# Background transfers of the state-space parameters on POOL's queue, and the kernel table's store one step later

## The chip, the cores and the metric

The kernel runs on one core of one Trainium2 chip. The time is device microseconds of one execution; the median of several runs is compared. The engines of the core are PE (matrix products), DVE and ACT (element-wise work), POOL (the GpSimd engine) and SP, whose only work here is to issue DMA transfers. Each engine has its own instruction queue and works through it in order; semaphores hold an instruction until what it needs is there.

## The reference

One step of a two-layer encoder for 512 prompt frames and 64 sample frames. Layer 0 has attention and a short convolution, layer 1 a diagonal state-space mixer (S5); each layer also has two SwiGLU blocks and a cross attention. The change touches only the parameters of the state-space mixer:

```python
def ssm_mixer(h, w_in, a_re, a_im, b_re, b_im, c_re, c_im, log_dt, d_skip, w_glu, h0_re, h0_im):
    u32 = (h @ w_in).astype(f32)
    ug = u32.reshape(B, S, SSM_GROUPS, SSM_GROUP)              # 64 groups of 16 channels
    lam = lax.complex(a_re, a_im)                              # (64 groups, 64 states)
    a_bar = jnp.exp(lam * jnp.exp(log_dt)[:, None])
    b_bar = ((a_bar - 1.0) / lam)[..., None] * lax.complex(b_re, b_im)
    c_mat = lax.complex(c_re, c_im)
    # h_t = a_bar * h_(t-1) + b_bar u_t ;  y_t = Re(c_mat h_t) + d_skip * u_t
    ...
    val, gate = jnp.split(jax.nn.gelu(y) @ w_glu, 2, axis=-1)
    return val * jax.nn.sigmoid(gate), h_last.real, h_last.imag
```

The kernel works through the frames in blocks of eight. For that it needs tables made of `a_bar`, `b_bar` and `c_mat` only: WIN (what eight inputs add to the state), T (what the inputs of a block give to the outputs of the same block, with `d_skip` on its diagonal), WOUT (what the state gives to eight outputs) and TAB (rotations). They do not depend on `x`.

## The kernel before

All activations lie feature by frame in SBUF, 576 frames wide. The work is a list of *steps* made by hand. A step names the weight pieces (granules) that it needs; `run_steps` issues the load of each granule on SP (`wraw`, three buffers, up to three ahead), lets ACT round it to a high part `wh` and DVE take the rest `wl`, and then emits the step's matrix products on PE, three passes of 128x288 each. A full granule is 512 KB.

Beside the steps runs a list of *background pieces*, `self.bg`. Each has a cost in microseconds; after every step, `run_steps` gives a credit of 6 per granule and emits pieces while credit is left. So the order of all instructions on every queue is fixed when the program is written; what an engine does at which time is settled by the semaphores alone.

`s5_params` makes the background pieces for the tables, during the first SwiGLU block:

- `start` and `to_rows` compute powers of `a_bar`; PE transposes them (L1518).
- The *WIN phase*: `win_load` brings factors `f` from a DRAM scratch, in 32 transfers of 128 KB (16 partitions each); `win_calc(i)`, for i from 0 to 7, loads `b` (512 KB, one buffer) and makes a complex product of six operations on POOL (L1402 to L1407), with the result in `w` (two buffers); `win_store` writes `w` to WIN in DRAM. The pools of this phase are closed at its end.
- The *kernel phase*: `ca_begin` opens new pools in the same memory, loads `x`, `bx` (four transfers of 512 KB, L1552 and L1553) and `dd`, and clears `gp`; `bst` makes the input matrix in `bx`. Then for each i: `ca_calc(i)` (POOL and DVE make `ca`), `local(i)` (PE multiplies, L1586; ACT copies into `gp`; DVE adds the diagonal), `ca_store` (WOUT) and `t_store` (eight transfers from shifted windows of `gp` to T).
- The rotation phase (TAB), on DVE and POOL.

Before the change every DMA of the kernel is issued by SP, the weight loads among them. A store to DRAM and a later load of memory that it read are tied by semaphores; each transfer uses one of eight semaphores of its kind, and waits until the transfer that used it eight transfers before has landed.

Of the kernel before, what the change touches and what calls it, by code (L numbers as in the profile page):

```python
# [9 lines left out]
F32 = mybir.dt.float32  # L10
# [67 lines left out]
class Kernel:  # L78
# [1305 lines left out]
    def s5_params(self):  # L1384

        nc, a = self.nc, self.a
        V, S_, P_ = nc.vector, nc.scalar, nc.gpsimd
        dr = self.dram
        d = self.s5d = {
            "F": dr.tile([2, 8, 4096], F32, name="s5f"),  # L1390
            "TAB": dr.tile([8, 128, 2 * 592], F32, name="s5tab"),
            "R8": dr.tile([128, SG], F32, name="s5r8"),
            "WIN": dr.tile([8, 128, 1024], F32, name="s5win"),
            "T": dr.tile([8, 128, 1024], F32, name="s5t"),
            "WOUT": dr.tile([8, 128, 1024], F32, name="s5wout"),
        }
        st = {}
# [3 lines left out]
        def cmul(e, o_r, o_i, ar, ai, br, bi, t):  # L1401
            e.tensor_tensor(o_r, ar, br, op=ALU.mult)  # L1402
            e.tensor_tensor(t, ai, bi, op=ALU.mult)
            e.tensor_tensor(o_r, o_r, t, op=ALU.subtract)
            e.tensor_tensor(o_i, ar, bi, op=ALU.mult)  # L1405
            e.tensor_tensor(t, ai, br, op=ALU.mult)
            e.tensor_tensor(o_i, o_i, t, op=ALU.add)  # L1407
# [115 lines left out]
        def win_load(hf, q):  # L1523
            if hf == 0 and q == 0:
                st["wp"] = self.phase_pool(st, "s5w")
                st["wp2"] = self.phase_pool(st, "s5w2", 2)
            if q == 0:
                st["f", hf] = [st["wp2"].tile([128, 32, G], F32, tag=f"f{c}", name="f") for c in range(2)]
            f, c = st["f", hf], q // 2
            for s in range(4 * (q % 2), 4 * (q % 2) + 4):  # L1530
                nc.sync.dma_start(f[c][16 * s:16 * s + 16].rearrange("p g n -> p (g n)"),
                                  d["F"][c, s:s + 1, hf * 2048:(hf + 1) * 2048].broadcast_to((16, 2048)))

        def win_calc(i):
            pl = st["wp"]
            b = pl.tile([128, 2, 8, G], F32, tag="b", name="b")
            nc.sync.dma_start(b, a["ssm_bw"][i].rearrange("p (c g n) -> p c g n", c=2, g=8))
            fr, fi = (f[:, (i % 4) * 8:(i % 4) * 8 + 8] for f in st["f", i // 4])
            w = st["w", i] = st["wp2"].tile([128, 8, 2, G], F32, tag="w", name="w")
            t = pl.tile([128, 8, G], F32, tag="t", name="t")  # L1540
            cmul(P_, w[:, :, 0], w[:, :, 1], b[:, 0], b[:, 1], fr, fi, t)

        def win_store(i):
            nc.sync.dma_start(d["WIN"][i], st["w", i].rearrange("p g c n -> p (g c n)"))


        def ca_begin():
            pl = st["wp"] = self.phase_pool(st, "s5o")
            st["x"] = [pl.tile([128, G, 16], F32, name=f"x{c}") for c in range(2)]
            st["bx"] = [pl.tile([128, G, 16], F32, name=f"bx{c}") for c in range(2)]  # L1550
            for c in range(2):
                nc.sync.dma_start(st["x"][c].rearrange("p g n -> p (g n)"), a["ssm_cx"][c])  # L1552
                nc.sync.dma_start(st["bx"][c].rearrange("p g n -> p (g n)"), a["ssm_bx"][c])  # L1553
            st["dd"] = pl.tile([16, G], F32, name="dd")
            nc.sync.dma_start(st["dd"], a["ssm_dd"])
            st["wp2"] = self.phase_pool(st, "s5o2", 2)
            st["gp"] = pl.tile([16, 8, 240], F32, name="gp")
            P_.memset(st["gp"], 0.0)

        def bst():  # L1560
            b0, b1 = st["bx"]
# [5 lines left out]
        def ca_calc(i):  # L1567
            pl = st["wp"]
            ca = st["ca", i] = st["wp2"].tile([128, 8, 9, 16], F32, tag="ca", name="ca")
            t = st["wp2"].tile([128, 8, 9, 16], F32, tag="cat", name="cat")  # L1570
            gs = slice(8 * i, 8 * i + 8)
            sh = (128, 8, 9, 16)
            x = [v[:, gs].unsqueeze(2).broadcast_to(sh) for v in st["x"]]
            p = [st["sr"][:, 9 * c:9 * c + 9, gs].rearrange("p k g -> p g k").unsqueeze(3).broadcast_to(sh) for c in range(2)]
            P_.tensor_tensor(ca, x[0], p[0], op=ALU.mult)
            V.tensor_tensor(t, x[1], p[1], op=ALU.mult)
            V.tensor_tensor(ca, ca, t, op=ALU.add)

        def ca_store(i):
            nc.sync.dma_start(d["WOUT"][i].rearrange("p (g n) -> p g n", g=8), st["ca", i][:, :, 1:].rearrange("p g k c -> p g (k c)"))  # L1580

        def local(i):
            ps = self.ps("ps_g")
            pf = ps[:16].rearrange("p b (g n) -> p (b g) n", g=4)
            for g in range(8):
                nc.tensor.matmul(pf[:, g], st["bx"][0][:, 8 * i + g], st["ca", i][:, g, 0:8].rearrange("p k c -> p (k c)"),  # L1586
                                 start=True, stop=True)
            gp = st["gp"]
            S_.activation(gp[:, :, 112:], pf, AF.Copy)
            dg = st["wp"].tile([16, 8, 16], F32, tag="dg", name="dg")  # L1590
            V.tensor_tensor(dg, self.ident[:16, :16].unsqueeze(1).broadcast_to((16, 8, 16)),
                            st["dd"][:, 8 * i:8 * i + 8].unsqueeze(2).broadcast_to((16, 8, 16)), op=ALU.mult)
            V.tensor_tensor(gp[:, :, 112:128], gp[:, :, 112:128], dg, op=ALU.add)

        def t_store(i):
            for s in range(8):
                nc.sync.dma_start(d["T"][i, 16 * s:16 * s + 16].rearrange("p (g n) -> p g n", n=128),
                                  st["gp"][:, :, 112 - 16 * s:240 - 16 * s])


        def rot_begin(hf):
# [36 lines left out]
        add = lambda cost, fn=lambda: None: pieces.append((cost, fn))  # L1638
# [9 lines left out]
        for hf in range(2):  # L1648
            if hf == 0:
                for q in range(4):  # L1650
                    add(2, lambda q=q: win_load(0, q))
            for i in range(4 * hf, 4 * hf + 4):
                add(8.6, lambda i=i: win_calc(i))
                if hf == 0:
                    add(0, lambda i=i: win_load(1, i))
                if i:
                    add(0, lambda i=i: win_store(i - 1))
        add(5)
        add(0, lambda: win_store(7))
        add(6)  # L1660
        add(2, lambda: (close(2), ca_begin()))
        add(20, bst)
        for i in range(9):
            if i < 8:
                add(5, lambda i=i: ca_calc(i))
            if i:
                add(5, lambda i=i: local(i - 1))
                add(0, lambda i=i: ca_store(i - 1))
                add(1, lambda i=i: t_store(i - 1))
        add(6)  # L1670
        add(2, lambda: close(2))
        for hf in range(2):
# [711 lines left out]
```

## Time and profile before

| | |
|---|---|
| Time, median of 3 runs | 2530.69 us (2527.84 to 2531.97) |
| Profiled execution: its time | 2536.29 us |
| Profiled execution: its span | 2534.3 us |
| PE busy | 2475.3 us (98%) |
| DVE busy | 1781.1 us (70%) |
| ACT busy | 1070.0 us (42%) |
| POOL busy | 764.1 us (30%) |
| Bytes moved, mean rate | 279.98 MB, 110 GB/s |
| Mean granted clock of PE | 0.989 |
| First issue of `f` / first WIN operation on POOL / last store of `w` landed | 115.58 / 138.07 / 228.0 us |

The profile is of one execution. *Busy* counts compute instructions; waiting and the issuing of transfers are not in it. A *wait* row names who waited, on which line, for whom. In a timeline row, what stands in brackets is the idle time of the engine ahead of the instruction, and what ended it. "SPq" is SP's queue of transfers, and the length that it shows for a transfer is that of its issue, not of the transfer.

### The profile page before, as it was taken

The page shows a single profiled execution, that of the slowest core. Times are in us where ns is not written, and L with a number is a line of the kernel's source. Part 1 is how long each engine was busy: PE and PEld are TensorE (multiplying, and loading weights), DVE is VectorE, ACT ScalarE, POOL GpSimd, SP SyncE. Part 2 cuts the span into 40 slices and gives each one's busy share as a digit, 9 for nine tenths or more (in the row PEclk, how much of TensorE's full clock was granted, in tenths as well). Part 3 has the DMA queues.
Part 4 walks back from the last instruction along what each step waited for, and adds up shares of the span by engine and source line. Part 5 has one row for each costly group of instructions (what it writes and reads, how often), then busy time and mean ns, then how long its engine had stood idle before and what let it go on. Part 6 is the DMA issues. An engine that isn't in the chain of part 4 may idle for free.

```text
span 2534.3 us, 45336 instructions
## 1 busy us (share of the span) xinstructions
PE 2475.3 (98%) x18499; PEld 2437.8 (96%) x18499; DVE 1781.1 (70%) x2680; ACT 1070.0 (42%) x1847; POOL 764.1 (30%) x754
## 2 busy tenths in 40 slices
PE   8998999999999999999989999999999999999998
PEld 8998999999899999999989999999999999999998
DVE  5644658667875588886988695965753468787695
ACT  5222222334655454443545352542453355444353
POOL 1566235302420051523334332412310005151431
PEclk9999999999999999999999999999999999999999
DMA  4375653321134322322221322244972222222221
GB/s 156 86 186 183 155 129 114 127 87 36 37 121 134 112 84 75 109 84 100 77 91 61 107 84 100 84 139 157 296 248 85 84 92 87 77 104 86 98 84 63
DMA packets 112560, 279.98 MB, mean 110 GB/s; under 512 B 16304, under 2 KB 45152, under 8 KB 111712
## 3 DMA queue, kind: packets, MB, share of 16 engines
q1 hardware_dynamic: 112352, 277.08, 34.3%
q8 instruction: 145, 2.38, 0.4%
q14 instruction: 63, 0.52, 0.1%
HBM read 245.07 MB, written 31.97 MB: 109 GB/s over the span
## 4 chain that ended last, share of the span: by engine, by line
PE 74%; DVE 13%; ACT 4%; DMA 4%; POOL 2%; issue 2%; SPq 1%; ACTq 0%; DVEq 0%; POOLq 0%
PE banks L396 35%; PE banks L317 26%; DVE wl L144 2%; DVE wl L219 2%; PE banks L657 2%; PE banks L1903 1%; PE banks L2179 1%; PE banks L1284 1%; PE banks L1799 1%; PE banks L1252 1%; ACT wh L138 1%; DMA b<-in_ssm_bw 1%; DMA u<-s5u 1%; DMA wraw<-in_gu 1%; POOL w L1405 1%
## 5 line engine op out<-in xcount | busy, mean ns | idle before, releaser
L138 ACT ACTIVATE wh<-wraw 128x1024 fp32r<-128x1024 f32 (+3 forms) x411 | 351.9, 860 | 330.5 <-PE banks L396 180.7
L219 DVE TENSOR_TENSOR wl<-wraw,wh 128x1024 fp32r<-128x1024 f32 (+2 forms) x264 | 335.4, 1274 | 179.6 <-ACT wh L138 177.4
L396 PE MATMUL banks<-hh,wh 128*128 128x288 f32 x1768 | 380.6, 297 | 2.6 <-ACT hh L138 1.8
L396 PE MATMUL banks<-hh,wl 128*128 128x288 f32 x1768 | 379.7, 296 | 2.5 <-DVE wl L219 2.5
L396 PE MATMUL banks<-hl,wh 128*128 128x288 f32 x1768 | 379.5, 296 | 0.3 <-DVE hl L144 0.3
L317 PE MATMUL banks<-xh,wh 128*128 128x288 f32 x1056 | 312.6, 296 | 0.1
L317 PE MATMUL banks<-xl,wh 128*128 128x288 f32 x1056 | 312.3, 296 | 0.2 <-DVE xl L146 0.2
L317 PE MATMUL banks<-xh,wl 128*128 128x288 f32 x1056 | 312.1, 296 | 0.0
L396 PEld LDWEIGHTS banks<-hh,wh 128*128 128x128 f32 x1768 | 285.8, 189 | 4.0 <-ACT hh L138 2.1
L396 PEld LDWEIGHTS banks<-hh,wl 128*128 128x128 f32 x1768 | 285.9, 189 | 3.0 <-DVE wl L219 3.0
L396 PEld LDWEIGHTS banks<-hl,wh 128*128 128x128 f32 x1768 | 285.8, 189 | 0.5 <-DVE hl L144 0.5
L396 PE MATMUL banks<-xh,wh 128*128 128x288 f32 x1232 | 268.3, 299 | 10.6 <-ACT wh L138 9.7
L396 PE MATMUL banks<-xh,wl 128*128 128x288 f32 x1232 | 266.0, 298 | 5.2 <-DVE wl L219 5.2
L396 PE MATMUL banks<-xl,wh 128*128 128x288 f32 x1232 | 265.1, 297 | 0.0
L317 PE MATMUL banks<-eh,wh 128*128 128x288 f32 x792 | 237.5, 300 | 17.6 <-ACT tb L138 16.7
L317 PE MATMUL banks<-el,wh 128*128 128x288 f32 x792 | 235.4, 297 | 0.0
L317 PE MATMUL banks<-eh,wl 128*128 128x288 f32 x792 | 235.2, 297 | 0.0
L144 DVE TENSOR_TENSOR wl<-ss,wh 128x512 fp32r<-128x512 f32 x264 | 197.3, 760 | 48.9 <-ACT wh L138 48.9
L292 POOL TENSOR_TENSOR ss<-raw 128x512 f32<-128x512 f32 x66 | 103.6, 1570 | 369.6 <-DMA raw<-in_gu 248.4
L396 PEld LDWEIGHTS banks<-xh,wh 128*128 128x128 f32 x1232 | 199.5, 190 | 13.0 <-ACT wh L138 10.2
L396 PEld LDWEIGHTS banks<-xh,wl 128*128 128x128 f32 x1232 | 199.7, 190 | 6.7 <-DVE wl L219 6.6
L317 PEld LDWEIGHTS banks<-xh,wh 128*128 128x128 f32 x1056 | 199.7, 189 | 0.4 <-ACT xh L140 0.4
(536 smaller groups left out, 5432.8 us busy)
## 6 DMA issues: line engine op xcount, KB each, us to landing
wraw<-in_gu SPq DMA_DIRECT2D x110, 512.0 KB
raw<-in_gu SPq DMA_DIRECT2D x66, 512.0 KB
wraw<-in_dn SPq DMA_DIRECT2D x64, 512.0 KB
wraw<-in_dn SPq DMA_DIRECT2D x32, 384.0 KB
wraw<-in_win SPq DMA_DIRECT2D x17, 512.0 KB
wraw<-in_xq SPq DMA_DIRECT2D x16, 512.0 KB
wraw<-in_xk SPq DMA_DIRECT2D x16, 512.0 KB
wraw<-in_xv SPq DMA_DIRECT2D x16, 512.0 KB
```

What stands on the lines that cost most here:

```text
L138: self.nc.scalar.activation(out, in_, AF.Copy)
L144: self.nc.vector.tensor_tensor(out, in_, hi.bitcast(F32), op=ALU.subtract)
L219: self.lo_engine.tensor_tensor(l[:p, :n], t[:p, :n], h[:p, :n].bitcast(F32), op=ALU.subtract)
L292: self.nc.gpsimd.tensor_tensor(t, x, y, op=op)
L317: mm(out, ww[:, ws], xx[:, kk], start=k < 3 and kk == 0 and pi == 0, stop=kk == 3 and pi == 2, skip_group_check=True)
L396: mm(ps[:M, h, :n], ww[:, k * M:(k + 1) * M], xx[:, k0 + k, h * n:(h + 1) * n], start=first and k == 0 and pi == 0, stop=last and k == kt ...
L657: nc.tensor.matmul(ps, ww[:, k * 128:(k + 1) * 128], xx[:, k, c0:c0 + n], start=k == 0 and pi == 0, stop=k == KT - 1 and pi == 2)
L1252: mm(out, x[:, k, t * 128:t * 128 + m], y[:, k], start=k == 0 and pi == 0, stop=k == 1 and pi == 2)
L1284: mm(out, x[:, k, f * 128:(f + 1) * 128], y[:, k, ts], start=k == 0 and pi == 0, stop=k == 1 and pi == 2)
L1405: e.tensor_tensor(o_i, ar, bi, op=ALU.mult)
L1799: mm(pv[:, m], x[:, kk, ms], y[:, k * MEM:(k + 1) * MEM], start=kk == m == pi == 0, stop=kk == 7 and pi == 2 and m == 1)
L1903: mm(ps[:, h, :HF], ww[:, k * 128:(k + 1) * 128], xx[:, k, h * HF:(h + 1) * HF], start=k == 0 and pi == 0, stop=k == 7 and pi == 2)
```

## The change

Three calls in the WIN phase are issued on POOL's queue and no longer on SP's: the loads of `f`, the loads of `b` and the stores of `w`. In the kernel phase there are two buffers `gp` in place of one, cleared both; `t_store(i)` is emitted one round of the loop later, after `ca_calc` of that round and ahead of the next `ca_store`; and `ca_store` is emitted ahead of `local` and no longer behind it.

```diff
 def win_load(hf, q):
-                nc.sync.dma_start(f[c][16 * s:16 * s + 16].rearrange("p g n -> p (g n)"),
+                nc.gpsimd.dma_start(f[c][16 * s:16 * s + 16].rearrange("p g n -> p (g n)"),
                                   d["F"][c, s:s + 1, hf * 2048:(hf + 1) * 2048].broadcast_to((16, 2048)))
 def win_calc(i):
-            nc.sync.dma_start(b, a["ssm_bw"][i].rearrange("p (c g n) -> p c g n", c=2, g=8))
+            nc.gpsimd.dma_start(b, a["ssm_bw"][i].rearrange("p (c g n) -> p c g n", c=2, g=8))
 def win_store(i):
-            nc.sync.dma_start(d["WIN"][i], st["w", i].rearrange("p g c n -> p (g c n)"))
+            nc.gpsimd.dma_start(d["WIN"][i], st["w", i].rearrange("p g c n -> p (g c n)"))
 def ca_begin():
-            st["gp"] = pl.tile([16, 8, 240], F32, name="gp")
-            P_.memset(st["gp"], 0.0)
+            st["gp"] = [pl.tile([16, 8, 240], F32, name=f"gp{c}") for c in range(2)]
+            for c in range(2):
+                P_.memset(st["gp"][c], 0.0)
 # local(i) and t_store(i) use st["gp"][i % 2]
-        for i in range(9):
+        for i in range(10):
             if i < 8:
                 add(5, lambda i=i: ca_calc(i))
-            if i:
+            if i > 1:
+                add(1, lambda i=i: t_store(i - 2))
+            if 0 < i < 9:
+                add(0, lambda i=i: ca_store(i - 1))
                 add(5, lambda i=i: local(i - 1))
-                add(0, lambda i=i: ca_store(i - 1))
-                add(1, lambda i=i: t_store(i - 1))
```

POOL's queue, from the third WIN step to the first operation of the fourth. DMAHW and DMASW are the semaphores of transfers issued by SP and by POOL; `s5win` is WIN in DRAM, `s5f` the scratch of the factors, `in_ssm_bw` the input that `b` is loaded from. Before:

```order
L1402 TENSOR_TENSOR w<-b,f 128x8x64 [waits DMAHW7_49,DMAHW6_49]
L1403 TENSOR_TENSOR t<-b,f 128x512 [waits Pool_49]
L1404 TENSOR_TENSOR w<-w,t 128x8x64 [waits Pool_49]
L1405 TENSOR_TENSOR w<-b,f 128x8x64
L1406 TENSOR_TENSOR t<-b,f 128x512 [waits Pool_49]
L1407 TENSOR_TENSOR w<-w,t 128x8x64 [waits Pool_49]
L1402 TENSOR_TENSOR w<-b,f 128x8x64 [waits DMAHW6_49,DMAHW5_49]
```

The step that begins with only the multiplication ahead of it has six more issues ahead of it now:

```order
L1407 TENSOR_TENSOR w<-w,t 128x8x64 [waits Pool_49]
L1531 DMA f<-s5f 16x2048 x3
L1531 DMA f<-s5f 16x2048 [waits DMASW1_49]
L1544 DMA s5win<-w 128x1024 [waits DMASW2_49]
L1537 DMA b<-in_ssm_bw 128x1024 [waits DMASW3_49]
L1402 TENSOR_TENSOR w<-b,f 128x8x64 [waits DMASW3_49,DMASW2_49]
```

Four loads of `f`, the store of the step before and the load of `b` stand between two steps on POOL; in the last steps, without `f`, there are two.

SP's queue at the passage from the WIN phase to the kernel phase (`in_gu` are weights, `in_ssm_cx` and `in_ssm_bx` the sources of `x` and `bx`). Before:

```order
L1544 DMA s5win<-w 128x1024 [waits Pool_49]
L1537 DMA b<-in_ssm_bw 128x1024 [waits DMAHW5_49,DMAHW0_49,Pool_49]
L188 DMA wraw<-in_gu 128x1024 [waits DMAHW2_49,DVE_49]
L1544 DMA s5win<-w 128x1024 [waits Pool_49]
L188 DMA wraw<-in_gu 128x1024 [waits DMAHW3_49,DVE_49]
L1544 DMA s5win<-w 128x1024 [waits DMAHW4_49,Pool_49]
L188 DMA wraw<-in_gu 128x1024 [waits DMAHW6_49,DVE_49]
L1552 DMA x_2274<-in_ssm_cx 128x1024 [waits DMAHW4_49,DMAHW7_49,DMAHW2_49,DMAHW0_49]
```

The same place now:

```order
L188 DMA wraw<-in_gu 128x1024 [waits DMAHW1_49,DVE_49]
L188 DMA wraw<-in_gu 128x1024 [waits DMAHW2_49,DVE_49]
L1552 DMA x_2274<-in_ssm_cx 128x1024 [waits DMASW4_49,DMASW3_49,DMASW5_49,DMASW2_49,DMASW6_49,DMASW1_49,DMASW7_49,DMASW0_49,Pool_49]
L1553 DMA bx_2276<-in_ssm_bx 128x1024
L1552 DMA x_2275<-in_ssm_cx 128x1024
L1553 DMA bx_2277<-in_ssm_bx 128x1024 [waits PE_49]
L1555 DMA dd<-in_ssm_dd 16x64
L188 DMA wraw<-in_gu 128x1024 [waits DMAHW3_49,DVE_49]
```

The weight loads ahead of L1552 wait for no transfer of the WIN phase any more, and L1552 itself waits for POOL and for all eight semaphores of POOL's transfers. The weight load behind L1552 stands where it stood.

More of the change, by code (lines that the diff above doesn't have):

```diff
@@ L1587, in local @@
                                  start=True, stop=True)
-            gp = st["gp"]
+            gp = st["gp"][i % 2]
             S_.activation(gp[:, :, 112:], pf, AF.Copy)
@@ L1597, in t_store @@
                 nc.sync.dma_start(d["T"][i, 16 * s:16 * s + 16].rearrange("p (g n) -> p g n", n=128),
-                                  st["gp"][:, :, 112 - 16 * s:240 - 16 * s])
+                                  st["gp"][i % 2][:, :, 112 - 16 * s:240 - 16 * s])
         def rot_begin(hf):
```

## The prediction

> **What bounds the kernel now.** I read the busy table and the chain of waits first, then the windows, then the timelines of SP and POOL where the windows show PE idle.
>
> ```profile
> span 2534.3 us, 45336 instructions
> ...
> PE 2475.3 (98%) x18499; PEld 2437.8 (96%) x18499; DVE 1781.1 (70%) x2680; ACT 1070.0 (42%) x1847; POOL 764.1 (30%) x754
> ...
> PE 74%; DVE 13%; ACT 4%; DMA 4%; POOL 2%; issue 2%; SPq 1%; ACTq 0%; DVEq 0%; POOLq 0%
> ```
>
> PE works 98% of the span, so only the 59 us in which it does not can be won. The changed code runs between 112 and 350 us. The windows there (length, then busy time of PE, PEld, DVE, ACT, POOL, then PE's granted clock, DMA share, GB/s):
>
> ```profile
> 120.00:128.00 8.00, 8.00 (x62) 8.00 (x62) 3.93 (x6) 1.91 (x2) 0.00 (x0) 1.00 1.00 130
> ...
> 165.00:185.00 20.00, 19.46 (x145) 19.10 (x144) 8.86 (x8) 4.07 (x5) 16.36 (x11) 1.00 0.71 215
> 185.00:205.00 20.00, 16.33 (x111) 15.85 (x110) 9.13 (x7) 4.57 (x6) 15.80 (x12) 0.91 0.48 162
> 205.00:225.00 20.00, 19.38 (x145) 19.10 (x144) 8.43 (x7) 5.35 (x7) 18.16 (x12) 1.00 0.40 141
> 225.00:245.00 20.00, 17.72 (x126) 17.49 (x125) 7.87 (x7) 4.78 (x6) 12.04 (x7) 0.95 0.75 263
> 245.00:350.00 105.00, 105.00 (x791) 100.59 (x790) 66.57 (x72) 25.52 (x28) 17.25 (x7) 0.99 0.60 139
> ```
>
> PE idles 0.54 + 3.67 + 0.62 + 2.28 = 7.1 us from 165 to 245, and not at all from 245 to 350. Clocks of 0.91 and 0.95 cost about 0.09 x 16.3 + 0.05 x 17.7 = 2.4 us more. So a perfect supply of weights here is worth 9.5 us, no more. What starves PE is seen on SP, which issues every transfer. Rows of its waits (us in total, times, longest), then of its timeline (start, length):
>
> ```profile
> SPq L1537 <- POOL t L1406: 52.4, 7, 7.8
> ...
> SPq L1544 <- POOL w L1407: 12.7, 4, 10.4
> ...
> 115.58 7.31 SPq L1531 DMA_DIRECT2D f<-s5f  x12
> ...
> 212.10 0.33 SPq L1537 DMA_DIRECT2D b<-in_ssm_bw  x1
> 212.52 0.38 SPq L188 DMA_DIRECT2D wraw<-in_gu  x1
> ```
>
> SP stands 52.4 us in front of the seven loads of `b` until POOL has read the one buffer of `b`; weight loads stand behind it. POOL's own rows, the first and the last step, and its waits:
>
> ```profile
> 138.07 1.29 POOL L1402 TENSOR_TENSOR w<-b,f 128x512 f32<-128x512 f32 x1 [34.95 <-DMA wraw<-in_gu]
> ...
> 222.85 2.26 POOL L1407 TENSOR_TENSOR w<-w,t 128x512 f32<-128x512 f32 x1
> ...
> POOL w L1402 <- DMA b<-in_ssm_bw: 12.8, 7, 2.4
> ```
>
> The eight steps last from 138.07 to 225.11, that is 87.0 us, of which the seven gaps between steps are 12.8 (1.8 each) and the arithmetic 74.2 (9.3 a step). A gap is so short because SP issues the next `b` while POOL still runs its last operation. Behind the last step the chain of waits, in order of time (start, length, what):
>
> ```profile
> 110.22 1.16 PE banks L1518 x16
> ...
> 212.10 3.20 DMA b<-in_ssm_bw
> ...
> 225.13 2.88 DMA s5win<-w
> 228.15 0.33 SPq L1552
> ...
> 230.73 7.11 DMA wraw<-in_gu
> 237.94 1.07 ACT wh L138
> 239.04 3.05 DVE wl L219
> 242.13 14.04 PE banks L396 x92
> 256.17 1.85 PE banks L1586 x16
> ```
>
> This is the hinge. When the last store of `w` has landed, at 228.0, SP may issue the loads of `x` (L1552), and only behind them the next weights. They reach PE at 242.13, 14.1 us after the store's landing.
>
> **The change, part by part.**
>
> *SP loses 48 transfers* (32 of `f`, 8 of `b`, 8 stores). Its waits for POOL go; the 14 weight loads ahead of L1552 follow DVE's use alone. PE would reach the work that now starts at 242.13 some 9.5 us earlier, at 232.6. But the changed SP order has L1552 waiting for POOL and all of POOL's transfers, and all later weights behind it. So PE starts that work at the later of 232.6 and (landing of the last store + 14.1). The gain exists only if the store lands by 218.5; each microsecond beyond 228.0 is a loss.
>
> *POOL gains 48 issues in its own order.* Nothing in this trace issues from POOL, so the price of one issue is bounded from both sides: SP's `b` issue takes 0.33 us, and POOL's operation on 128x512 takes 1.29 us, at its dearest 2.28 (below). I take 1.0, nearer to POOL's row because POOL itself spends the time.
>
> ```profile
> L1405 POOL TENSOR_TENSOR w<-b,f x8: 1295/2276/2291, 141.9 to 219.2; 128x512 f32<-128x512 f32 x8
> ```
>
> The Trainium skill, "DMA: Bandwidth & Descriptors", Specifications, gives the first byte of a GpSimd-issued transfer about 1 us against 0.6 us from SP. By that, an estimate, the same sum with 0.4 us more for each of eight loads of `b` and nothing else would be 3 us slower; no row here shows it.
>
> *First step.* `f` can be issued when the transposes and their copies are done, at about 112 (L1518 row), 3.6 us before SP's first. From 120 to 128 only `f` moved: 130 GB/s at a DMA share of 1.00, so one `f` (131 kB) keeps all sixteen engines for 1.0 us. Sixteen of them and `b` need 17 us of issue or about as much of transfer; with 3.5 us for `b` to land the first step starts at 112 + 17 + 3.5 = 132.5, I say 133, 5 us earlier than now.
>
> *The gaps.* POOL now issues the next `b` only after its last operation, and behind four `f` and a store in the same queue. Gap one (four `f`, `b`): 5 issues, and 3.5-4 to land, 9 us. Gaps two to four (with a store ahead, which moves as many bytes as `b`): 6 issues and 4.5, 10.5 each. Gaps five to seven (store, `b`): 2 issues and 4, 6 each. Landing starts from the row of 3.20 us, plus the bytes queued ahead. Sum 9 + 31.5 + 18 = 58.5 us instead of 12.8.
>
> *Arithmetic.* 74.2, less 4.5: the last three steps would run while PE and so DVE have nothing to do, and L1405 then takes 1.29 and not 2.28, other rows alike (1.5 a step).
>
> *End.* One store issue 1.0 and landing 2.9 (row 225.13).
>
> Sum: 133 + 69.7 + 58.5 + 3.9 = 265.1 against 228.0: the store lands 37 us later, and PE stands from about 233 to 265.1 + 14.1 = 279.2 instead of starting at 242.1. The idle PE returns with one slow-clock spell; it has one at 242 already, so I add nothing.
>
> *Order of `ca_store`, `local` and `t_store`; two `gp`.* One wait goes, ACT's for the store of `gp`:
>
> ```profile
> 269.85 1.02 ACT L1589 ACTIVATE gp<-banks 16x1024 f32<-16x1024 f32 x1 [9.78 <-DMA s5t<-gp]
> ...
> SPq L1597 <- DVE gp L1593: 33.5, 8, 8.4
> ```
>
> PE is busy 105.00 of 105 us there, so the 9.8 us of ACT and the 33.5 us of SP are worth nothing now; what hides them is weights already prepared, and if that cover shrank they would be worth at most a part of the 9.8. The second memset of `gp` costs POOL one more 1.7 us, beside the landing of `bx`, for which POOL waits anyway:
>
> ```profile
> 228.15 1.69 POOL L1558 MEMSET gp<- 16x1920 f32 x1 [3.04 <-DMA s5win<-w]
> 233.64 1.94 POOL L1563 TENSOR_TENSOR bx<-bx,sr 128x1024 f32<-128x1024 f32 x1 [3.80 <-DMA bx<-in_ssm_bx]
> ```
>
> PE's own wait behind this, L1586 at 256.17, moves along with everything else. Zero for this part; bounds -1 and +2.
>
> The whole: 37 us. The profiled execution took 2536.29 us around its span of 2534.3 and is 5.6 above the median of 2530.69; on the median the sum gives 2568.
>
> **The rivals.**
>
> *Cheap issues.* If POOL issues as fast as SP, 0.33, the `f` transfers still bind: first step 130.5, gaps 1 + 4 + 1.3 + 1.5 = 7.8, three of 9.1, three of 4.3, together 48; end 3.2. Landing at 130.5 + 69.7 + 48 + 3.2 = 251.4: 23 us slower, 2554. If `f` did not delay `b` at all (gaps 4.9, 5.2, 3.9), 235 and +7, 2538. For it speaks that SP's row is the only one of an issue; against it, that POOL has no help.
>
> *Dear issues.* At 1.7 us: first step 144.4, gaps 12 + 41 + 24.6, end 4.6, landing 296.4: +68, 2599. At 2.28: +96, 2627. It speaks for this that POOL's operations double whenever DVE is beside them.
>
> *Faster.* SP's 52.4 us of standing is what starves PE; without it PE runs through and 9.5 us are gained, 2521. This decides if the last store lands by 218.5. With arithmetic of 74.2 and an end of 3.2 that leaves 218.5 - 77.4 - 112 = 29 us for sixteen `f`, nine landings and 48 issues; the `f` alone take 16. I see no row that lets it.
>
> *No change that can be told.* Gains and losses cancel when the store lands at about 228, 38.6 us for the same list: issues must be almost free and every `b` land as fast as now. 2531. The Trainium skill, "DMA: Bandwidth & Descriptors", Rules for kernel authors, says that spreading transfers over issuing engines brings no bandwidth and saves only the sequencer's issue time. By that the transfers would run as now; the trace bears it out for the engines being shared (1.00 busy with `f` alone), but not for the order of issue, which is what I price.
>
> **How the numbers follow.** Forecast 58%, cheap issues 15%, dear 19%, faster 5%, no change 3%. Time: 2568. The range leaves out the faster and the unchanged (8%) and the dearer half of the dear (about 9%): from 2543, between the two sums for cheap issues, to 2600, at 1.7 us an issue. A change under 0.2% (5 us) is about what a measurement of this kernel cannot tell from none. Slower 0.92, same 0.03, faster 0.05.
>
> **What the changed profile would show.** No PE idle from 165 to about 230, then one gap of 30 to 45 us ended by a weight load issued right behind L1552; SP's longest wait at L1552 for POOL or for the store of `w`; POOL's steps starting near 133, then 18 to 20 us apart for four and 15 for three; 245 to 350, moved by the same amount, as full as before. I am wrong if POOL's issues lie beside its arithmetic, or if the gaps stay near 2 us.

## The result, and the profile after

The changed kernel takes 2570.26 us (median of four runs, 2568.52 to 2571.67), the kernel before 2531.33 us on the same chip (2527.84 to 2533.19). The ratio is 1.015, with a 95% interval of 1.0137 to 1.0163: 38.9 us slower.

The page of the changed kernel: its span and busy times.

```profile
span 2568.4 us, 45336 instructions
...
PE 2470.0 (96%) x18499; PEld 2432.5 (95%) x18499; DVE 1786.0 (70%) x2680; ACT 1068.6 (42%) x1847; POOL 782.0 (30%) x803
```

PE does the same 18499 products in 2470.0 us, but the span has grown: it stands still for longer. The windows show where (columns as in the windows of before):

```profile
120.00:128.00 8.00, 8.00 (x62) 8.00 (x61) 4.00 (x6) 1.91 (x2) 2.50 (x5) 1.00 1.02 162
128.00:140.00 12.00, 12.00 (x92) 12.00 (x91) 6.43 (x7) 2.13 (x2) 1.20 (x1) 1.00 0.95 237
...
165.00:185.00 20.00, 20.00 (x152) 20.00 (x152) 9.26 (x8) 4.91 (x6) 12.01 (x13) 1.00 0.55 158
...
225.00:235.00 10.00, 6.91 (x52) 6.67 (x51) 0.00 (x0) 0.00 (x0) 7.87 (x7) 0.97 0.10 41
235.00:245.00 10.00, 0.00 (x0) 0.00 (x0) 0.00 (x0) 0.00 (x0) 5.80 (x7) 0.50 0.28 105
245.00:265.00 20.00, 0.00 (x0) 0.00 (x0) 0.00 (x0) 0.00 (x0) 11.97 (x12) 0.50 0.28 105
265.00:285.00 20.00, 7.04 (x37) 6.69 (x38) 8.06 (x4) 2.69 (x3) 15.47 (x7) 0.57 0.59 210
...
300.00:390.00 90.00, 90.00 (x682) 86.14 (x681) 55.27 (x60) 22.24 (x24) 11.61 (x5) 1.00 0.66 148
```

Up to 225 PE runs without a break and at full clock, which it did not before. Then comes one hole, from about 232 to 276, in which PE does nothing, and until 275 neither do DVE and ACT; only POOL works. PE makes four products at 276.2, works without a break from 279.3 and is full again from there. The waits from 100 to 300 us give the length (us in total, times, longest):

```profile
ACT wh L138 <- DMA wraw<-in_gu: 59.8, 2, 54.5
POOL w L1402 <- DMA b<-in_ssm_bw: 49.0, 8, 11.9
...
PE banks L396 <- ACT wh L138: 44.3, 1, 44.3
```

PE's one wait of 44.3 us stands at the end of a chain that starts on POOL: eight waits for the landing of `b`, 49.0 us (11.9 of them ahead of the first step), where the seven gaps had 12.8 before. SP's waits in the same stretch show where the two are joined:

```profile
SPq L1552 <- DMA s5win<-w: 65.3, 3, 52.8
```

SP had issued its last free weight load by 198 and then stood at L1552 until the last store of `w` had landed. The chain of waits behind that store, in order of time:

```profile
260.90 4.24 DMA s5win<-w
...
265.22 0.33 SPq L1552
...
267.79 7.21 DMA wraw<-in_gu
...
275.11 1.06 ACT wh L138
...
276.19 3.05 DVE wl L219
...
279.29 13.83 PE banks L396 x92
293.12 1.85 PE banks L1587 x16
```

The store lands at 265.14, and PE restarts 14.15 us later, at 279.29. Before, the same two events stood at 228.0 and 242.13: the same 14.1 us apart, and 37.2 us earlier. The two spans differ by 34.1 us only, because the profiled execution of before lost time in another place. Its windows and those of the second experiment below, which has the same work there:

```profile
1750.00:2000.00 250.00, 243.16 (x1883) 241.80 (x1884) 136.82 (x164) 94.53 (x132) 51.73 (x73) 0.97 0.58 188
```

```profile
1750.00:2000.00 250.00, 243.23 (x1928) 241.38 (x1928) 141.62 (x171) 96.06 (x135) 51.70 (x73) 1.00 0.60 195
```

At a granted clock of 0.97 the first made 45 products fewer in the same busy time, some 6 us of work, about the 5.6 us by which it stood above the median of before. The changed kernel made 1907 products at a clock of 0.99 in the same stretch of its work, 1787 to 2037. That is 24 more than the profiled execution of before, some 3 us, and about the 3.1 us by which 34.1 falls short of 37.2.

### The profile page after: what moved, and what is told of

Its sections match the earlier page's. It is cut to its first block, busy times and chain, and to the rows that moved or that the text cites. A ratio compares the mean times of both kernels' runs of the same rounds, so it can differ in the third digit from the quotient of the medians.

```text
span 2568.4 us, 45336 instructions
## 1 busy us (share of the span) xinstructions
PE 2470.0 (96%) x18499; PEld 2432.5 (95%) x18499; DVE 1786.0 (70%) x2680; ACT 1068.6 (42%) x1847; POOL 782.0 (30%) x803
## 4 chain that ended last, share of the span: by engine, by line
PE 73%; DVE 13%; ACT 4%; DMA 4%; POOL 3%; issue 2%; SPq 0%; ACTq 0%; DVEq 0%; POOLq 0%
PE banks L396 35%; PE banks L317 26%; DVE wl L144 2%; DVE wl L219 2%; PE banks L1905 2%; PE banks L657 2%; DMA b<-in_ssm_bw 2%; PE banks L1801 1%; PE banks L1284 1%; PE banks L1252 1%; ACT wh L138 1%; PE banks L2181 1%; PE banks L1587 1%; DVE mx L990 1%; DVE xl L146 1%
## 5 line engine op out<-in xcount | busy, mean ns | idle before, releaser
L396 PEld LDWEIGHTS banks<-xh,wh 128*128 128x128 f32 x1232 | 200.4, 191 | 54.1 <-ACT wh L138 51.5
L396 PEld LDWEIGHTS banks<-xl,wh 128*128 128x128 f32 x1232 | 200.7, 191 | 0.1
```

Source lines behind the costliest of these rows:

```text
L396: mm(ps[:M, h, :n], ww[:, k * M:(k + 1) * M], xx[:, k0 + k, h * n:(h + 1) * n], start=first and k == 0 and pi == 0, stop=last and k == kt ...
```

## The experiments

My theory: the time follows the landing of the last store of `w`, and this landing is late because POOL issues `b` in its own queue and then stands bare until `b` has landed. Rivals: the table's store and the two `gp` cost part of it; the price of the issues, not the wait for `b`, makes the steps long; or SP's stand at L1552, not POOL, is what must go. The kernels of the first four sections ran on one chip (before: 2531.63 us), those of the last four on another (before: 2533.11 us). A difference is taken to the median of before on the same chip.

### The queue alone

Before, with the three calls on POOL's queue and nothing else:

```diff
-nc.sync.dma_start(f[c][16 * s:16 * s + 16]...
+nc.gpsimd.dma_start(f[c][16 * s:16 * s + 16]...
-nc.sync.dma_start(b, a["ssm_bw"][i]...
+nc.gpsimd.dma_start(b, a["ssm_bw"][i]...
-nc.sync.dma_start(d["WIN"][i], st["w", i]...
+nc.gpsimd.dma_start(d["WIN"][i], st["w", i]...
```

> Only the queue of f, b and the stores of w is changed; order of the table's stores and the single gp are as before. Theory (the last store of w lands late on POOL's queue, and SP holds the weights behind L1552 until then): the whole loss is here, 2570 us, 36 to 41 over before; store of w landed near 265. Rival (part of the loss comes from t_store one step later, which holds weights on SP behind eight more waits): under 2565.

2567.59 us, 36.0 more than before (ratio 1.0144, 1.013 to 1.0158). Its chain:

```profile
260.58 4.23 DMA s5win<-w
...
279.02 14.00 PE banks L396 x92
```

The landing at 264.8 and the restart at 279.0 are those of the whole change. The three calls make nearly all of the loss, 36.0 of 38.9 us. The two intervals (33 to 40 and 35 to 41 us) overlap, and a few microseconds for the rest of the change are not excluded.

### The table's store and two buffers alone

The changed kernel with the same three calls back on `nc.sync`; two `gp`, the later `t_store` and the order of `ca_store` stay.

```diff
-nc.gpsimd.dma_start(f[c][16 * s:16 * s + 16]...
+nc.sync.dma_start(f[c][16 * s:16 * s + 16]...
-nc.gpsimd.dma_start(b, a["ssm_bw"][i]...
+nc.sync.dma_start(b, a["ssm_bw"][i]...
-nc.gpsimd.dma_start(d["WIN"][i], st["w", i]...
+nc.sync.dma_start(d["WIN"][i], st["w", i]...
```

> Only the two gp, t_store one round later and ca_store ahead of local; all transfers on SP. Theory: PE is full from 245 to 350 us, so nothing is won or lost: ratio 1.000 within 0.001, 2529 to 2534. Rival (ACT's wait of 9.8 us for the store of gp delays weights that PE wants): 2 to 6 us faster.

2533.86 us, 2.2 more (ratio 1.0009, 1.0000 to 1.0018). ACT's wait for the store of `gp`, 9.8 us at its longest before, is gone from the rows of this kernel, and PE does as much as before from 245 to 350:

```profile
245.00:350.00 105.00, 105.00 (x788) 100.61 (x788) 70.89 (x73) 25.79 (x30) 16.45 (x7) 0.99 0.60 139
```

The wait that this part removes cost nothing, since PE was 105.00 us busy there with it too. The part is worth at most a loss of 4.6 us, and not a measurable gain.

### Two buffers of `b`, all on SP

If SP's wait for `b` is what starves PE, a second buffer takes it away without another queue:

```diff
 # the kernel before
-            b = pl.tile([128, 2, 8, G], F32, tag="b", name="b")
+            b = st["wp2"].tile([128, 2, 8, G], F32, tag="b", name="b")
```

> The kernel before with one change: b comes from a pool of two buffers, so that SP need not wait for POOL's reading of the previous b. Theory: the gaps between WIN steps fall from 12.8 us in all to under 3, the last store lands by about 218, and the 9.5 us that PE loses between 165 and 245 come back: 2520 to 2524. Rival (SP still stands in front of the stores of w for POOL, and the weights behind it starve PE as now): 2528 to 2532.

2520.31 us, 11.3 less (ratio 0.9959, 0.9945 to 0.9972): faster than both kernels. Its windows:

```profile
185.00:205.00 20.00, 20.00 (x152) 20.00 (x152) 10.57 (x8) 4.91 (x6) 19.69 (x14) 1.00 0.53 175
...
225.00:245.00 20.00, 20.00 (x151) 19.81 (x151) 17.72 (x13) 5.45 (x7) 8.46 (x4) 1.00 0.43 131
```

PE has no idle time left, and POOL works 19.69 of 20 us: its steps stand back to back. The timeline of POOL at its end (in brackets the idle time ahead, and what ended it):

```profile
210.33 2.15 POOL L1407 TENSOR_TENSOR w<-w,t 128x512 f32<-128x512 f32 x1
215.51 1.69 POOL L1558 MEMSET gp<- 16x1920 f32 x1 [3.03 <-DMA s5win<-w]
```

The last product of `w` is done at 212.5, and its store has landed by 215.5, three microseconds ahead of the 218.5 that the prediction asked for, and the whole gain of a perfect supply is there (9.5 forecast, 11.3 measured with an interval of 7 to 14). This run alone does not say what brought it, since SP's waits for `b` are gone as well as the later landing. The changed kernel helps to part the two: freed of the same waits, its PE had no idle time up to 225 either, though its store landed at 265. So what PE wins ahead of 225 comes from SP's order, and only what it wins behind 225 can come from the landing.

### `b` one step ahead, on POOL

The changed kernel, with two buffers of `b`, and the `b` of step i+1 issued before the arithmetic of step i.

```diff
-            b = pl.tile([128, 2, 8, G], F32, tag="b", name="b")
-            nc.gpsimd.dma_start(b, a["ssm_bw"][i]...
+            for j in ((0, 1) if i == 0 else (i + 1,)):
+                if j < 8:
+                    st["b", j] = st["wp2"].tile([128, 2, 8, G], F32, tag="b", name="b")
+                    nc.gpsimd.dma_start(st["b", j], a["ssm_bw"][j]...
+            b = st["b", i]
```

> The changed kernel with two buffers b, each b issued on POOL one step before it is used, so ahead of the arithmetic of the step before. Theory (the loss is the landing of b, which stands bare between two steps): of the gaps only the issues remain, 2.5 + 3 x 3.1 + 3 x 1.1 = 15 us; first step 139, arithmetic 74, end 5: store landed at 233, 5 us later than before, 2536 (2530 to 2542). Rival (transfers issued by POOL are slow in themselves, or their issue holds POOL): the gaps stay at 5 us and more, 2555 or later.

2553.94 us, 22.3 more than before (ratio 1.009, 1.0076 to 1.0104). It takes away 16.6 of the 38.9 us, half of what I expected. Its waits tell why:

```profile
POOL w L1402 <- DMA s5win<-w: 21.1, 6, 5.5
```

Between steps POOL no longer waits for `b`; now it waits for the store of `w`. Step i writes the buffer from which step i-2 was stored, and that store is issued on POOL only behind the arithmetic of step i-1, so right ahead of the step that needs it to have landed. I had not seen this second wait, which the load of `b` had covered.

### `b` back on SP

The changed kernel with one call moved back, and one buffer of `b` as in it:

```diff
-nc.gpsimd.dma_start(b, a["ssm_bw"][i]...
+nc.sync.dma_start(b, a["ssm_bw"][i]...
```

> The changed kernel with b back on SP; f and the stores of w stay on POOL. Theory: SP issues b while POOL runs its last operation, so a gap is the larger of POOL's own issues (2.0 to 2.5 us with f, 0.6 without) and the landing of b less 1.5 to 2.3: about 2.5 each with f, 2 without, 16 in all; the last store lands near 231 to 236: 3 to 8 us slower than before, 2537 (2530 to 2545). Rival (whatever POOL issues costs, f above all with 32 of 48 issues): 2555 or later.

2570.66 us, 37.6 more than before (ratio 1.0152, 1.0138 to 1.0166): no gain at all, against an expected 2537. Its waits:

```profile
POOL w L1402 <- DMA s5win<-w: 40.5, 6, 8.4
...
POOL w L1402 <- DMA b<-in_ssm_bw: 11.5, 2, 11.2
```

Only the first two steps wait for `b`; the other six wait for the store instead, nearly as long in all. From the fifth step to the sixth on POOL:

```profile
209.25 1.26 POOL L1407 TENSOR_TENSOR w<-w,t 128x512 f32<-128x512 f32 x1
210.45 0.60 POOL L1544 DMA_DIRECT2D s5win<-w  x1
217.86 1.28 POOL L1402 TENSOR_TENSOR w<-b,f 128x512 f32<-128x512 f32 x1 [6.81 <-DMA s5win<-w]
```

SP had issued a `b` at 209.19 and two weight loads right behind it. The store of 210.45 took 7.34 us to land beside them; the store of the same step in the kernel with `b` ahead, issued at 210.12, took 3.13. That SP's transfers delay it is likely, but was not tested by itself. SP also stands in front of `b` for POOL again, 81.5 us in seven waits, and PE starves long ahead of the last landing (the changed kernel was 20.00 us busy in this window):

```profile
185.00:205.00 20.00, 15.42 (x97) 14.90 (x97) 4.52 (x5) 2.43 (x3) 12.68 (x13) 0.84 0.43 105
```

PE's restart still stands 13.3 us behind the landing. The wait for `b` and that for the store are two locks on the same door, and here the second held when the first was opened.

### `b` ahead, and the store right behind its own step

The kernel with `b` ahead, and `w` stored one step earlier:

```diff
-                if i:
-                    add(0, lambda i=i: win_store(i - 1))
+                add(0, lambda i=i: win_store(i))
 ...
-        add(0, lambda: win_store(7))
```

> As the kernel with b one step ahead on POOL (2553.9 us), but each store of w is issued right behind its own step and no longer behind the next. There the bare landing of b was replaced by a wait of the product for the store of w that used its buffer two steps before (3.0 to 6.6 us a step). Theory: with the store issued 12 us earlier that wait goes too, and only issues are left between steps: 15 us in all, last store landed at 231, 2535 (2530 to 2541). Rival (POOL's issues and their transfers hold the next step in another way): 2545 or later.

2541.92 us, 8.8 more than before (ratio 1.0036, 1.0023 to 1.0048). POOL's timeline where a step follows a step:

```profile
172.93 1.29 POOL L1407 TENSOR_TENSOR w<-w,t 128x512 f32<-128x512 f32 x1
174.16 1.99 POOL L1531 DMA_DIRECT2D f<-s5f  x4
176.14 0.56 POOL L1547 DMA_DIRECT2D s5win<-w  x1
176.70 0.53 POOL L1539 DMA_DIRECT2D b<-in_ssm_bw  x1
177.25 1.30 POOL L1402 TENSOR_TENSOR w<-b,f 128x512 f32<-128x512 f32 x1
...
231.97 0.60 POOL L1547 DMA_DIRECT2D s5win<-w  x1 [0.41 <-POOL w L1407]
```

Between steps both waits are gone, and only the issues remain: 3.0 us from the end of a step to the start of the next with four `f`, 1.1 to 1.6 without. The last store leaves at 231.97 and lands at 234.92, against 231 expected; the time is 1 us over the expected range. With 30 of the 38.9 us taken away it is still slower than before, where SP makes all these issues beside POOL's arithmetic. Of the 6.9 us by which its store still lands later than before, the gaps make half: 16.3 us against 12.8. The arithmetic is 76.0 us against 74.2, the first step starts 1.2 us later, and the end is 0.5 longer.

### Half the loads of `f`

The changed kernel without the loads of `f` for steps 4 to 7, which use the factors of the first half; so half of the `f` traffic and 16 of POOL's issues are left out.

```diff
-                if hf == 0:
-                    add(0, lambda i=i: win_load(1, i))
-            fr, fi = (... for f in st["f", i // 4])
+            fr, fi = (... for f in st["f", 0])
```

> The changed kernel without the 16 loads of f for the second half (the last four steps multiply by the first half's factors; WIN is then not the reference's). Theory (f is ahead of b in the same queue and so in the gap): gaps one to four, 8.0 + 10.9 + 8.7 + 8.3, become 4.7 and three of 5.3; 15 us less, 2555 (2551 to 2559). Rival (f is beside other work, b alone counts): 2565 to 2570.

2558.63 us, 25.5 more than before (ratio 1.0104, 1.0089 to 1.0119). Chain and waits:

```profile
250.25 3.76 DMA s5win<-w
```

```profile
POOL w L1402 <- DMA b<-in_ssm_bw: 46.3, 8, 11.9
```

The landing moves 11.1 us forward, to 254.0. The 16 issues alone are 16 x 0.49 = 8 us of that; the rest is a shorter wait for `b`. The gaps between steps, read off the starts of L1402, sum to 41.3 us against 51.9; the first four, which lost their `f`, make 23.5 against 35.9 (20.6 expected). The time lies in the expected range and outside the rival's: the `f` stand in the gap.

### The loads of `x` and `bx` on POOL too

The changed kernel with `x`, `bx` and `dd` issued by `nc.gpsimd`, so that SP has nothing to wait for at L1552 and its weights go on:

```diff
-nc.sync.dma_start(st["x"][c]...
+nc.gpsimd.dma_start(st["x"][c]...
-nc.sync.dma_start(st["bx"][c]...
+nc.gpsimd.dma_start(st["bx"][c]...
-nc.sync.dma_start(st["dd"], a["ssm_dd"])
+nc.gpsimd.dma_start(st["dd"], a["ssm_dd"])
```

> The changed kernel with the loads of x, bx and dd moved to POOL's queue too, so that no weight load on SP stands behind L1552. Theory: PE no longer stops for weights, but it runs only some 14 us further, to the first product with bx and ca (local), which needs the same late end of the WIN phase: store landed at 265, bx there by 270, local ready near 288 where it now starts at 293: 2564 (2558 to 2568), with PE waiting for DVE's ca and no more for weights. Rival (the loss is SP's order alone): 2520 to 2530.

2572.7 us (2564.26 to 2575.37; ratio 1.0154, 1.0136 to 1.0173): not to be told from the changed kernel, and over the expected range. PE's stop did not vanish, it changed its cause. Its waits from 225 to 300, and the end of its chain:

```profile
PE banks L396 <- ACT hh L138: 45.5, 1, 45.5
```

```profile
276.71 2.34 POOL bx L1566
279.05 2.21 POOL ca L1576
...
284.58 1.21 DVE wl L219
285.79 0.68 DVE td L638
...
286.49 0.69 ACT hh L138
...
287.23 2.12 PE banks L396 x6
```

The weights came, but `ca_calc` has two operations on DVE that stand in DVE's queue ahead of `td` (L638), from which PE's next operand is made. The first reads `x`, and the second POOL's `ca`:

```profile
273.08 1.76 DVE L1577 TENSOR_TENSOR cat<-x,sr 128x1152 f32<-128x1152 f32 x1 [42.51 <-DMA dd<-in_ssm_dd]
281.28 3.38 DVE L1578 TENSOR_TENSOR ca<-ca,cat 128x1152 f32<-128x1152 f32 x1 [6.44 <-POOL ca L1576]
```

The profiled run of this kernel is its fastest, at 2564.26, and lies in the expected range; the others are as slow as the changed kernel, so a gain of a few microseconds stays open. SP's stand at L1552 is not the only lock at this place either.

### All of them together

| kernel | last store landed | against 228.0 | time against before |
|---|---|---|---|
| two `b` on SP | 215.5 | -12.5 | -11.3 |
| table only | 228.8 | +0.8 | +2.2 |
| `b` ahead, store at once | 234.9 | +6.9 | +8.8 |
| `b` ahead | 248.4 | +20.4 | +22.3 |
| half of `f` | 254.0 | +26.0 | +25.5 |
| queue only | 264.8 | +36.8 | +36.0 |
| whole change | 265.1 | +37.1 | +38.9 |
| `b` back on SP | 266.1 | +38.1 | +37.6 |

Over 50 us of landing the time follows within 2 us. In every row but the first PE stops, and restarts 13.2 to 14.2 us behind the landing; in the first it does not stop, and part of its gain is SP's. The kernel with `x` on POOL is left out: its store landed at 265.0 in a run of 2564.26 us (+31.2), its median is +39.6, and there DVE's queue hands the delay on.

## Why the prediction was right, and where its steps were off

**The hinge held.** L1552 and all later weights wait for the last store of `w`, and PE restarts 14.1 us behind its landing (14.15 measured; 13.2 to 14.2 in the seven kernels of the table in which PE stops). "Each microsecond beyond 228.0 is a loss" was found in them; and in the one kernel whose store lands ahead of 218.5 the gain is there and PE does not stop. The slow-clock spell that I added nothing for cost nothing more: the first 92 products behind the stop took 13.83 us, against 14.04 before.

**The sum, term by term.** Forecast and measured, in us: first step 133 / 138.8; arithmetic 69.7 / 69.65; the seven gaps 58.5 / 51.9; end 3.9 / 4.8; landing 265.1 / 265.14. The total is right to a tenth because the terms' errors cancel, not because each was right. POOL's rows show the parts:

```profile
138.81 1.93 POOL L1402 TENSOR_TENSOR w<-b,f 128x512 f32<-128x512 f32 x1 [11.87 <-DMA b<-in_ssm_bw]
...
165.06 1.98 POOL L1531 DMA_DIRECT2D f<-s5f  x4
167.04 0.56 POOL L1544 DMA_DIRECT2D s5win<-w  x1
167.59 0.54 POOL L1537 DMA_DIRECT2D b<-in_ssm_bw  x1
175.96 1.82 POOL L1402 TENSOR_TENSOR w<-b,f 128x512 f32<-128x512 f32 x1 [7.83 <-DMA b<-in_ssm_bw]
...
260.30 1.14 POOL L1544 DMA_DIRECT2D s5win<-w  x2
```

- *Price of an issue.* I took 1.0 us; it is 0.50 for `f`, 0.54 for `b` and 0.56 to 0.60 for a store. By price alone the rival of cheap issues was the nearer one (0.33). That POOL spends the time itself, and does nothing else meanwhile, was right.
- *Landing of `b`.* I took 3.5 to 4.5 us. From the start of its issue to the next step it is 8.4 in the gap above and 4.7 to 5.0 in the last ones, where only a store is ahead. So part of what I charged to the issue is the landing. In the gap above the DMA engines were 0.91 to 1.14 busy in each microsecond from 167 to 175. They moved 2.6 MB from 165 to 176, of which POOL's four `f`, store and `b` are 1.57; the rest is about the two weight loads that SP issued at 166.2 and 171.7. So what held `b` there is mainly the bytes moved with it and ahead of it. The Trainium skill, "DMA: Bandwidth & Descriptors", Anatomy of one DMA, fits a transfer issued from GpSimd by 2.0 us plus its bytes at 436 GB/s; for a store and a `b` taken as one transfer (1.05 MB) that makes, as an estimate, 4.4 us. The trace has 5.2 us from the store's issue to the landing in the last gap (247.4 to 252.6) and agrees roughly, but the fit knows nothing of four `f` ahead.
- *First step.* 5.8 us later than forecast. The issues were done at 126.9, two microseconds earlier than I had it, yet `b` took 11.8 us from there to land. I had it land in 3.5 us, as on an idle queue. The windows from 120 to 140 show the DMA engines 1.02 and 0.95 busy: SP, freed of its `f`, had put its weights beside POOL's transfers. I also misread the trace of before: from 120 to 128 not only `f` moved, as SP issued a weight load at 123.61. A price of 1.0 us for one `f` held even so: from 122.4 to 126.4 POOL issues one each 1.0 us, as the transfer eight places ahead of it lands. The place of `b` behind `f` in the queue is not what held the first step: in the kernel with `b` back on SP it was issued at 119.86, 6.5 us earlier, and the first step started only 1.8 us earlier, at 137.0. In all ten kernels it starts at 135.7 to 139.3, whoever issues `f` and `b`. With the DMA engines 1.00 to 1.04 busy from 120 to 136, before and after, that points at the bytes to be moved and not at the issues; how much of it is the weights' was not separated.
- *Gaps.* 8.0, 10.9, 8.7, 8.3, 5.5, 5.2 and 5.3 us where I had 9, three of 10.5 and three of 6. (In the rival of dear issues I wrote 77.6 for the gaps; with the landings of the forecast they make 78.8.)
- *Arithmetic.* Right, and for its reason: DVE had nothing to do from 220 on, and the last three steps took 7.6 to 7.7 us, the five ahead of them 9.0 to 10.2.
- *End.* The last two stores leave together (the row of 260.30, x2), so twice the bytes land at the end: 4.8 us against 3.0 for the single last store of the kernel with the store at once. I had counted one.

**A step that I did not have.** I named one wait that the gap consists of, that for `b`. The store of `w` in POOL's queue makes a second one, hidden behind the first: 21.1 us in the kernel with `b` ahead, 40.5 in that with `b` on SP. The queue shown with the change names it already, since L1402 waits there for two semaphores, that of `b` (DMASW3) and that of the store (DMASW2). The forecast for the whole change did not suffer, since both run side by side; my expectations for the two kernels that removed the first alone, 2536 and 2537, failed on it by 18 and 34 us.

**What hides what.** The table's part at zero held within its interval (+2.2, 0.0 to 4.6), though the median lies just over the upper bound of 2 that I gave it. The cover that I named, weights already prepared for a PE that is 105.00 us busy, is in the rows of that kernel as before.

**The rule on issuing engines.** The Trainium skill, "DMA: Bandwidth & Descriptors", Issuing engines are not separate DMA queues, has it that another engine saves only the sequencer's time to initiate, usually a small thing. Here SP's time was saved and PE did run without idle time to 225, as its windows show. But the issues were put into the queue of an engine whose arithmetic is the path: 3.0 us a step with four `f`, even with every landing between steps hidden.

## What to carry to other kernels

A transfer issued by a compute engine starts only when that engine's queue reaches it; if the same engine then needs the data, the whole landing lies bare, so such a move needs the load one step ahead and the store right behind its producer (and cost 8.8 us here even so), or it only exchanges a wait on an idle engine for one on the path. Where SP stands for a buffer, give the buffer a twin first: one changed line gained 11.3 us here, where the new queue alone lost 36.0. Before removing a wait, ask what else the waiting instruction waits for: a wait row names only the last releaser, and the list of semaphores in the instruction's own row names them all.

## What the runs showed of the hardware that I had not expected

An issue of a transfer on POOL took 0.48 to 0.60 us whether it moved 128 or 512 KB, in POOL's in-order time, against 0.32 to 0.44 us for most of SP's issues of `b`, `w`, `x`, `bx` and the weights. A store of 512 KB issued from POOL with nothing ahead of it landed 2.95 us after the start of its issue, as fast as from SP (2.86 in the kernel with the table's part alone). So the long landings of stores belong to what moved around them, not to POOL as the issuer; for the loads of `b` this is inferred, as no run here shows one issued by POOL with nothing beside it. While PE stood idle from 235 to 265, its granted clock read 0.50.
